# The S5 matrix to the state, formed from transposed and repeated factors

## The chip, the core and the metric

The kernel runs on one core of one Trainium2 chip. The metric is the device time of one execution in microseconds. Below, TensorE is PE (its weight loads PEld), VectorE is DVE, ScalarE is ACT, GpSimd is POOL, and SP is the engine whose queue issues most of the loads.

## The reference, cut to what matters

The program is one step of a two-layer backbone (D 1024, 128 context and 256 latent tokens). Each layer is a feed-forward block (FFN), a mixer of three branches, and a second FFN. One branch of the mixer is a bidirectional S5 layer: 32 groups of 16 channels, 64 complex states per group and direction.

```python
def _s5_direction(u, a_re, a_im, log_dt, b_re, b_im, c_re, c_im, h0, reverse):
    dt = jnp.exp(log_dt)[:, None]
    mag = jnp.exp(a_re * dt)
    abar_r, abar_i = mag * jnp.cos(a_im * dt), mag * jnp.sin(a_im * dt)
    ...
    bbar_r = qr[..., None] * b_re - qi[..., None] * b_im
    bbar_i = qr[..., None] * b_im + qi[..., None] * b_re
    bu_r = jnp.einsum('gph,blgh->blgp', bbar_r, u)
    ...
    _, _, sr, si = lax.associative_scan(_ssm_combine, (ar, ai, bu_r, bu_i), reverse=reverse, axis=1)
    y = jnp.einsum('ghp,blgp->blgh', c_re, sr) - jnp.einsum('ghp,blgp->blgh', c_im, si)
```

## The kernel before

The S5 layer is computed in chunks of TC = 8 steps. Per group it needs three small matrices that depend on the weights alone: ms, from the 8 x 16 inputs of a chunk to the 128 state values (64 states, two directions; real and imaginary part apart), my, from the state to the chunk's outputs, and mi, from the chunk's inputs directly to its outputs. The element of ms for step j, channel h and state s is abar(s) to a power that depends on j, times bbar(s, h). The mixer loads ms with steps and channels (j, h) on the partitions.

These tables are made by a generator, `tables(l)`, that runs beside the first FFN of its layer. Every matrix product of the program is a sequence of weight units (512 rows x 256 columns). After each unit `tick()` advances the tracks: `tables(0)` by 1.9 steps a tick from the eighth tick on, `tables(1)` by 1.6. A step ends at a `yield`. What a step issues on PE stands in PE's queue behind the unit at which it came, since PE's order is written out by hand; the orders of the other engines and queues are set by a planner when the program is built.

`s5_params` runs once, for both layers: it forms pw, the powers 0 to 8 of abar, and writes to DRAM (px_d) two selections of them, one for ms (L866 to L881). `s5_tables(l)` loads both (psx, pyx), runs `s5_rotations`, and then takes four blocks of GB = 8 groups. A block transposes cr to cT on PE, forms bb (bbar, states on the partitions) and two padded copies of operands. It then takes its groups in two halves of GS = 4. For each half VectorE forms my by six operations on 128 x 512 elements and mt, which is ms with the states on the partitions, by another six (L1008 to L1017). Three empty steps follow. Then PE multiplies my with bp and bb (the responses of the chunk, L1024 and L1034, copied to kall), transposes mt eight times (L1047, L138) to tb banks, and ScalarE copies these to ms (L1050), which POOL's queue writes to ms_d. At the block's end kall goes to DRAM, is read in shifted form as mib and written as mi. All DMAs of the tables are issued by POOL's queue; the tiles rotate through the pools c4 (5 buffers), c2 (7) and s1 (7).

A weight unit is loaded by SP's queue to wr, one of 3 buffers (L149), copied by ScalarE to its rounded part wh (L126) and subtracted by VectorE to the low part wl (L105, a line that all two-operand VectorE operations share); wh and wl have 3 buffers each. Three multiplications per tile (L198 to L200) use them. The tracks also load modulation weights modw by SP's queue, which PE multiplies at L386.

Of the kernel before, what the change touches and what calls it, by code (L numbers as in the profile page):

```python
# [56 lines left out]
def hybrid_step(ctx: ExitStack, tc: tile.TileContext, I, pos_r, pos_c, y_prompt, y_sample, new_state):  # L57
# [661 lines left out]
    px_d = [drm.tile([P, 2, 2, TC, G], F32, tag=f"px{l}", name=f"px{l}") for l in range(DEPTH)]  # L719
# [68 lines left out]
    def s5_params(raw, ldt):  # L788
# [81 lines left out]
        lo_i = slice(TC - 1, None, -1), slice(1, TC + 1)  # L870
        hi_i = slice(0, TC), slice(TC, 0, -1)
        for w in range(2):
            px = c4([P, DEPTH, 2, TC, G], "px")
            for i in range(2):
                for rows, ix in ((LO, lo_i[w]), (HI, hi_i[w])):
                    src = pw[rows, i, ix, :].rearrange("p n (l g) -> p l n g", l=DEPTH)
                    for l in range(DEPTH):
                        act.activation(px[rows, l, i], src[:, l], AF.Copy)
            for l in range(DEPTH):
                q.dma_start(px_d[l][:, w], px[:, l])  # L880
# [43 lines left out]
    def s5_tables(l):  # L924
        q = nc.gpsimd
        px = []
        for w in range(2):
            t = c2([P, 2, TC, G], "pxl")
            q.dma_start(t, px_d[l][:, w])
            px.append(t)  # L930
        psx, pyx = px
# [12 lines left out]

        nxt = load_bc(0)
        yield
# [3 lines left out]
        for gb in range(G // GB):  # L950
# [8 lines left out]
            bb = c2([P, 2, GB, 2 * H], "bb")  # L959
            pool.memset(bb, 0.0)  # L960
# [4 lines left out]
            bp = c2([P, 2, GB, 2 * H], "bp")  # L965
            pool.memset(bp, 0.0)
# [4 lines left out]
            ts_(nci, cT[:, 1], -1.0)  # L971
            if gb + 1 < G // GB:
                nxt = load_bc(gb + 1)
            kall = s1([P, 2, 9 * H], "kall")
            for sb in range(GB // GS):
                s0 = sb * GS

                def pexp(tab, i):
                    v = tab[:, i, :, g0 + s0 : g0 + s0 + GS]
                    return v.rearrange("p n g -> p g n").unsqueeze(3).to_broadcast(sh)  # L980
# [5 lines left out]
                b_r, b_i = vec(bb[:, 0]), vec(bb[:, 1])  # L986
                my = c4([P, GS, 2, TC, H], "my")
                t1, t2 = c2(sh, "tp1"), c2(sh, "tp2")
                mul(t1, pexp(pyx, 0), c_r)
                mul(t2, pexp(pyx, 1), c_i)  # L990
# [3 lines left out]
                mul(t1, pexp(pyx, 1), c_r)  # L994
                yield
                mul(t2, pexp(pyx, 0), c_i)
# [21 lines left out]
                for _ in range(3):  # L1018
                    yield
# [830 lines left out]
```

## Time and profile before

| | us |
|---|---|
| median of 3 runs | 1777.1 |
| lowest, highest | 1776.47, 1781.04 |
| time of the profiled execution | 1782.77 |
| its span in the trace | 1780.7 |
| PE busy in the span | 1746.5 |
| DVE, ACT, POOL busy | 1247.1, 794.0, 202.8 |
| bytes moved by DMA | 344.48 MB |

Busy times are unions over one engine's instructions; a matmul's end is modelled and overlaps with the next one's start, so the sum of a group's busy times can be more than what the group adds to the time. In the groups of instructions the number behind the x is the count, then come the busy time and the mean of one, then the idle time of the engine just before them and what ended it. In the timeline a row can merge several instructions in a row of one kind (x8).

### The profile page before, as it was taken

To read this page: it belongs to the slowest core of one execution; us is meant where nothing else is said; L and a number is where in the kernel's file an instruction comes from. 1 tells how busy PE (TensorE), PEld (TensorE's weight loads), DVE (VectorE), ACT (ScalarE), POOL (GpSimd) and SP (SyncE) were. 2 spreads that over 40 slices of the span, in tenths; PEclk is the share of its full clock that TensorE was granted. 3 is DMA by queue.
4 is the path that set the end of the run, shared out by engine and by line. 5 is a ranking of instruction groups with operands and counts; after the bars stand their busy time and mean duration, and the time that the engine had idled before them with its cause. 6 is when DMAs were issued, how large, how long until landed. Compare 5 with 4: busy or idle time off the path is not lost.

```text
span 1780.7 us, 30944 instructions
## 1 busy us (share of the span) xinstructions
PE 1746.5 (98%) x12116; PEld 1654.8 (93%) x12116; DVE 1247.1 (70%) x2344; ACT 794.0 (45%) x1330; POOL 202.8 (11%) x400
## 2 busy tenths in 40 slices
PE   7999999999999999999999999999999999999997
PEld 4899999999899989999999899999989999999997
DVE  4496776778987786679387656767799777544435
ACT  3344333475355553233357233336734646423333
POOL 2012343410010000000001133232100000000000
PEclk8999999999999999999999999999999999999999
DMA  9778788776744577778346777667666443443442
GB/s 329 249 227 273 226 251 270 226 199 185 250 145 131 166 229 224 251 267 265 114 127 208 229 226 213 181 194 232 166 206 195 124 131 119 130 130 121 129 124 77
DMA packets 253753, 344.48 MB, mean 193 GB/s; under 512 B 22399, under 2 KB 216651, under 8 KB 253608
## 3 DMA queue, kind: packets, MB, share of 16 engines
q1 hardware_dynamic: 228504, 299.18, 53.5%
q0 software_dynamic: 17088, 39.51, 7.3%
q10 hardware_dynamic: 8016, 3.82, 0.8%
q8 instruction: 95, 1.56, 0.4%
q14 instruction: 50, 0.41, 0.1%
HBM read 309.75 MB, written 32.70 MB: 192 GB/s over the span
## 4 chain that ended last, share of the span: by engine, by line
PE 84%; DVE 8%; DMA 3%; ACT 3%; issue 1%; SPq 0%; ACTq 0%; DVEq 0%
PE mm L198 26%; PE mm L199 25%; PE mm L200 25%; PE ax L386 3%; DVE wl L105 2%; DVE m_t L105 1%; PE tb L138 1%; DMA modw<-in_w_mod_dram 1%; DVE cacc L123 1%; DVE m_hh L105 1%; PE tb L1249 1%; ACT wh L126 1%; DMA wr<-in_w_in_dram 1%; DMA wr<-in_w_gate_dram 1%; DVE macc L123 1%
## 5 line engine op out<-in xcount | busy, mean ns | idle before, releaser
L105 DVE TENSOR_TENSOR wl<-wr,wh 128x1024 fp32r<-128x1024 f32 (+2 forms) x389 | 457.1, 1176 | 359.8 <-ACT wh L126 354.9
L126 ACT ACTIVATE wh<-wr 128x1024 fp32r<-128x1024 f32 (+1 forms) x387 | 395.5, 1022 | 619.0 <-PE mm L199 452.8
L198 PE MATMUL mm<-hh,wh 128*128 128x384 f32 x1840 | 626.8, 341 | 4.0 <-ACT hh L621 4.0
L200 PE MATMUL mm<-hh,wl 128*128 128x384 f32 x1840 | 617.8, 336 | 1.8 <-DVE wl L105 1.8
L199 PE MATMUL mm<-hl,wh 128*128 128x384 f32 x1840 | 617.4, 336 | 0.2
L198 PEld LDWEIGHTS mm<-hh,wh 128*128 128x128 f32 x1840 | 346.7, 188 | 33.3 <-issue 18.1
L200 PEld LDWEIGHTS mm<-hh,wl 128*128 128x128 f32 x1840 | 346.7, 188 | 3.1 <-DVE wl L105 3.1
L199 PEld LDWEIGHTS mm<-hl,wh 128*128 128x128 f32 x1840 | 346.8, 188 | 1.4 <-DVE hl L105 1.0
L198 PE MATMUL mm<-ah,wh 128*128 128x384 f32 x800 | 271.9, 340 | 0.0
L199 PE MATMUL mm<-al,wh 128*128 128x384 f32 x800 | 269.7, 337 | 1.7 <-DVE al L105 1.7
L200 PE MATMUL mm<-ah,wl 128*128 128x384 f32 x800 | 269.3, 337 | 0.0
L198 PEld LDWEIGHTS mm<-ah,wh 128*128 128x128 f32 x800 | 150.2, 188 | 9.9 <-issue 6.7
L199 PEld LDWEIGHTS mm<-al,wh 128*128 128x128 f32 x800 | 150.2, 188 | 2.0 <-DVE al L105 2.0
L200 PEld LDWEIGHTS mm<-ah,wl 128*128 128x128 f32 x800 | 150.1, 188 | 0.0
L123 DVE SCALAR_TENSOR_TENSOR x<-mm,gt,x 128x128 f32<-128x128 f32 x224 | 83.1, 411 | 33.0 <-PE mm L200 32.7
L198 PE MATMUL mm<-xh,wh 128*128 128x386 f32 x240 | 84.8, 353 | 0.0
L126 ACT ACTIVATE ah<-av 128x384 fp32r<-128x384 f32 x82 | 42.1, 518 | 91.7 <-DVE av L105 91.3
L200 PE MATMUL mm<-xh,wl 128*128 128x386 f32 x240 | 82.1, 342 | 0.0
L199 PE MATMUL mm<-xl,wh 128*128 128x386 f32 x240 | 82.0, 342 | 0.0
L123 DVE SCALAR_TENSOR_TENSOR macc<-modw,silu_c,macc 128x1024 f32<-128x1024 f32 x56 | 69.9, 1278 | 13.8 <-DMA modw<-in_w_mod_dram 13.8
L123 DVE SCALAR_TENSOR_TENSOR cacc<-pad,pv,cacc 128x399 f32<-128x399 f32 x120 | 68.6, 625 | 0.0
L386 PE MATMUL ax<-modw,silu_c 128*32 128x512 f32 (+1 forms) x576 | 62.6, 514 | 0.4 <-DMA modw<-in_w_mod_dram 0.4
(316 smaller groups left out, 1820.4 us busy)
## 6 DMA issues: line engine op xcount, KB each, us to landing
wr<-in_ffn_w_dram SPq DMA_DIRECT2D x256, 512.0 KB, 3.6
modw<-in_w_mod_dram SPq DMA_DIRECT2D x144, 512.0 KB, 5.0
wr<-in_w_gate_dram SPq DMA_DIRECT2D x48, 512.0 KB, 4.3
wr<-in_w_in_dram SPq DMA_DIRECT2D x24, 512.0 KB, 3.6
my<-my POOLq DMA_DIRECT2D x16, 512.0 KB, 5.5
ms<-ms POOLq DMA_DIRECT2D x16, 512.0 KB, 4.9
m_ms<-ms SPq DMA_DIRECT2D x16, 512.0 KB, 4.7
m_my<-my SPq DMA_DIRECT2D x16, 512.0 KB, 10.6
```

The source lines that it names most:

```text
L105: (eng or dve).tensor_tensor(out, a, b, op=op)
L123: dve.scalar_tensor_tensor(out, a, s, b, op0=op0, op1=op1)
L126: act.activation(hi, full, AF.Copy)
L138: pe.transpose(out, in_, ident[:rows, :rows])
L198: pe.matmul(out, wh[:, k, cols], xh, start=first, stop=False)
L199: pe.matmul(out, wh[:, k, cols], xl, start=False, stop=False)
L200: pe.matmul(out, wl[:, k, cols], xh, start=False, stop=last)
L386: pe.matmul(b[32 * s : 32 * s + 32, :w], silu_c[:, k, :], raws[i][:, c : c + w], start=(k == 0), stop=(k == KD - 1), skip_group_check=True,)
L1249: pe.matmul(b[64 * half : 64 * half + NCH, g * P : (g + 1) * P], u, w, start=(n == 0), stop=(n == 2), skip_group_check=True,)
```

## The change

ms is no longer formed with the states on the partitions and transposed on PE per half block. Its two factors are transposed instead: the powers once (pw, in `s5_params`, eight transposes), and bbar once per block (bc, two transposes, `factor_rows`). Both are written to DRAM (pt_d, bt_d) and repeated there by DRAM-to-DRAM copies to the rows (j, h): the powers over the channels (ptr_d, four copies in `s5_params`), bbar over the steps (btr_d, one copy per block). Each half block loads its 4 groups of both (pt, bt) and VectorE forms ms directly, by six operations on 128 x 512 elements. px_d holds only the selection for my. The steps of a block are reordered: both halves' my first, the responses of the first half during the second half's my, then the two loads, the responses of the second half, and the two halves of ms. The clears of bb and bp (`padded`) move one block ahead. The steps of a block are 16 instead of 17; `s5_params` has four more.

```diff
-    px_d = [drm.tile([P, 2, 2, TC, G], F32, ...
+    px_d = [drm.tile([P, 2, TC, G], F32, ...
+    pt_d = [drm.tile([2, TC, G, P], F32, ...
+    bt_d = [drm.tile([H, G, 2, P], F32, ...
+    ptr_d = [drm.tile([TC, H, 2, G * P], F32, ...
+    btr_d = [drm.tile([TC, H, G, 2 * P], F32, ...
...
+        pws = c4([P, TC, P], "pws")
+        for i in range(2):
+            b = tb_bank()
+            for m in range(TC // 2):
+                transpose(
+                    b[:, m * P : (m + 1) * P], pw[:, i, 2 * m : 2 * m + 2, :].rearrange("p n r -> p (n r)"), P
+                )
+            bv = b.rearrange("p (m s) -> p m s", s=P)
+            o = pws[:, 4 * i : 4 * i + 4]
+            act.activation(o[:, ::-1, LO], bv[:, :, LO], AF.Copy)
+            act.activation(o[:, :, HI], bv[:, :, HI], AF.Copy)
+            yield
+        for n2 in range(2):
+            for l in range(DEPTH):
+                r = n2 * NG + l * G
+                rows_d = pt_d[l].rearrange("i j g s -> (i j) g s")
+                for half, off in ((LO, 1 - n2), (HI, n2)):
+                    q.dma_start(
+                        rows_d[off::2, :, half].rearrange("m g s -> g m s"), pws[r : r + G, :, half]
+                    )
+        yield
+        for l in range(DEPTH):
             for i in range(2):
+                src = pt_d[l][i].rearrange("j g s -> j (g s)").unsqueeze(1).to_broadcast([TC, H, G * P])
+                q.dma_start(ptr_d[l][:, :, i], src)
         yield
...
+        def padded():
+            t = [c2([P, 2, GB, 2 * H], nm) for nm in ("bb", "bp")]
+            for v in t:
+                pool.memset(v, 0.0)
+            return t
...
+            bc = s1([P, 2, GB, H], "bc")
+            act.activation(bc, bb[:, :, :, :H], AF.Copy)
...
+            def factor_rows():
+                b = tb_bank()
+                for i in range(2):
+                    transpose(b[:, i * P : (i + 1) * P], bc[:, i].rearrange("p g h -> p (g h)"), P)
+                bts = s1([P, 2, P], "bts")
+                act.activation(bts.rearrange("p i s -> p (i s)"), b[:, : 2 * P], AF.Copy)
+                q.dma_start(bt_d[l][:, gs].rearrange("h g i s -> g h (i s)"), bts.rearrange("r i s -> r (i s)"))
+                src = bt_d[l][:, gs].rearrange("h g i s -> h g (i s)").unsqueeze(0)
+                q.dma_start(btr_d[l][:, :, gs], src.to_broadcast([TC, H, GB, 2 * P]))
...
-                mt = c4([P, GS, 2, TC, H], "mt")
-                t1, t2 = c2(sh, "tp1"), c2(sh, "tp2")
-                mul(t1, pexp(psx, 0), b_r)
...
-                for _ in range(3):
-                    yield
...
+            def to_rows_in(sb):
+                gr = slice(g0 + sb * GS, g0 + (sb + 1) * GS)
+                pt = c4([P, 2, GS * P], "pt")
+                cols_ = slice(gr.start * P, gr.stop * P)
+                q.dma_start(pt, ptr_d[l].rearrange("j h i x -> (j h) i x")[:, :, cols_])
+                bt = c4([P, GS, 2 * P], "bt")
+                q.dma_start(bt, btr_d[l].rearrange("j h g x -> (j h) g x")[:, gr])
...
+            def to_rows(sb):
+                pt, bt = ins[sb]
+                ms = c4([P, GS, 2, P], "ms")
+                t1, t2 = (c2([P, GS, P], f"tp{i}") for i in (1, 2))
+                mul(t1, pt[:, 0], bt[:, :, 0])
+                mul(t2, pt[:, 1], bt[:, :, 1])
                 yield
+                sub(ms[:, :, 0], t1, t2)
+                t1, t2 = (c2([P, GS, P], f"tp{i}") for i in (1, 2))
+                mul(t1, pt[:, 0], bt[:, :, 1])
                 yield
+                mul(t2, pt[:, 1], bt[:, :, 0])
+                add(ms[:, :, 1], t1, t2)
+                q.dma_start(ms_d[l][:, g0 + sb * GS : g0 + (sb + 1) * GS], ms)
+                yield
...
-                ms = c4([P, GS, 2, P], "ms")
-                for g2 in range(0, GS, 2):
-                    b = tb_bank()
-                    for j in range(4):
-                        transpose(
-                            b[:, j * P : (j + 1) * P], mt[:, g2 + j // 2, j % 2].rearrange("p i h -> p (i h)"), P
-                        )
-                    act.activation(ms[:, g2 : g2 + 2].rearrange("p g r c -> p (g r c)"), b, AF.Copy)
-                q.dma_start(ms_d[l][:, g0 + s0 : g0 + s0 + GS], ms)
+            mys, ins = [], []
+            yield
+            for n, _ in enumerate(from_rows(0)):
+                if n == 1:
+                    factor_rows()
+                yield
+            for n, _ in enumerate(from_rows(1)):
+                if n == 0:
+                    responses(0)
+                yield
+            to_rows_in(0)
+            yield
+            to_rows_in(1)
+            yield
+            responses(1)
+            if gb + 1 < G // GB:
+                pads = padded()
+            yield from to_rows(0)
+            yield from to_rows(1)
```

## Rows read from the trace of the kernel before

**Rows 1.** The page: busy PE, and the span in 40 slices of 44.5 us.

```profile
PE 1746.5 (98%) x12116; PEld 1654.8 (93%) x12116; DVE 1247.1 (70%) x2344; ACT 794.0 (45%) x1330; POOL 202.8 (11%) x400
DMA  9778788776744577778346777667666443443442
GB/s 329 249 227 273 226 251 270 226 199 185 250 145 131 166 229 224 251 267 265 114 127 208 229 226 213 181 194 232 166 206 195 124 131 119 130 130 121 129 124 77
```

**Rows 2.** The page: the chain that ended last, by engine, shares of the span.

```profile
PE 84%; DVE 8%; DMA 3%; ACT 3%; issue 1%; SPq 0%; ACTq 0%; DVEq 0%
```

**Rows 3.** Stretches of 10 us: busy PE, PEld, DVE, ACT, POOL, clock, DMA, GB/s.

```profile
140.00:150.00 10.00, 10.00 (x60) 8.91 (x59) 4.37 (x8) 6.14 (x10) 4.89 (x13) 1.00 0.98 337
150.00:160.00 10.00, 10.00 (x61) 8.91 (x60) 2.77 (x3) 3.08 (x5) 0.00 (x0) 1.00 1.04 385
230.00:240.00 10.00, 10.00 (x59) 10.00 (x58) 8.93 (x15) 3.16 (x5) 3.11 (x6) 1.00 1.04 394
```

**Rows 4.** Waits: who waited for whom; us in total, times, longest.

```profile
SPq L149 <- DVE wl L105: 1085.9, 324, 8.0
ACT wh L126 <- PE mm L199: 452.8, 217, 5.1
```

**Rows 5.** Chain in order of time near 350 us: start us, us, what.

```profile
350.35 10.31 DMA wr<-in_w_in_dram
```

**Rows 6.** Timeline, one burst of table matmuls: start us, duration us, engine, line.

```profile
182.27 0.34 PE L200 MATMUL mm<-hh,wl 128*128 128x384 f32 x1
182.54 0.65 PE L1024 MATMUL tb<-my,bp 128*32 128x128 f32 x16
183.22 1.24 PE L138 MATMUL tb<-ident,mt 128*128 128x128 f32 x8
184.22 0.42 PE L198 MATMUL mm<-hh,wh 128*128 128x384 f32 x1
```

**Rows 7.** Groups of instructions, whole span: busy us, mean ns of one, idle before.

```profile
L138 PE MATMUL tb<-ident,mt 128*128 128x128 f32 x128 | 19.3, 287 | 0.0
L1050 ACT ACTIVATE ms<-tb 128x512 f32<-128x512 f32 x32 | 17.9, 598 | 2.5 <-PE tb L138 2.5
L105 DVE TENSOR_TENSOR mt<-tp,tp 128x512 f32<-128x512 f32 x32 | 21.9, 685 | 0.2
L105 DVE TENSOR_TENSOR tp<-pxl,bb 128x512 f32<-128x512 f32 x64 | 42.5, 685 | 0.4
L958 ACT ACTIVATE cT<-tb 128x256 f32<-128x256 f32 x8 | 2.9, 368 | 0.9 <-PE tb L138 0.9
```

**Rows 8.** Timeline around the transposes that begin a block of eight groups.

```profile
162.93 0.34 PE L200 MATMUL mm<-hh,wl 128*128 128x384 f32 x1
163.10 0.38 PE L138 MATMUL tb<-ident,cr 128*128 128x128 f32 x2
163.24 0.42 PE L198 MATMUL mm<-hh,wh 128*128 128x384 f32 x1
```

**Rows 9.** Timeline of POOL, before the first block of layer 0.

```profile
124.35 0.71 POOL L938 DMA_DIRECT2D braw<-in_s_b_re_dram  x1
127.64 0.56 POOL L929 DMA_DIRECT2D pxl<-px  x1 [2.58 <-DMA px<-px]
```

**Rows 10.** Timeline, VectorE and ScalarE: the first output matrix of that block.

```profile
164.09 0.37 ACT L958 ACTIVATE cT<-tb 128x256 f32<-128x256 f32 x1
165.97 1.89 DVE L105 TENSOR_TENSOR tp<-pxl,cT 128x512 f32<-128x512 f32 x3
171.02 0.68 DVE L123 SCALAR_TENSOR_TENSOR my<-tp,tp 128x512 f32<-128x512 f32 x1
```

**Rows 11.** DMA issues: count, KB each, median us from issue to landing.

```profile
my<-my POOLq DMA_DIRECT2D x16, 512.0 KB, 5.5
m_my<-my SPq DMA_DIRECT2D x16, 512.0 KB, 10.6
mib<-kd POOLq DMA_DIRECT2D x64, 64.0 KB, 5.2
```

More of the change, by code (lines that the diff above doesn't have):

```diff
@@ L718, in hybrid_step @@
     rho_d = [drm.tile([P, 4, G // 4, NE], F32, tag=f"rhod{l}", name=f"rhod{l}") for l in range(DEPTH)]
-    px_d = [drm.tile([P, 2, 2, TC, G], F32, tag=f"px{l}", name=f"px{l}") for l in range(DEPTH)]
+    px_d = [drm.tile([P, 2, TC, G], F32, tag=f"px{l}", name=f"px{l}") for l in range(DEPTH)]
+    pt_d = [drm.tile([2, TC, G, P], F32, tag=f"pt{l}", name=f"pt{l}") for l in range(DEPTH)]
+    bt_d = [drm.tile([H, G, 2, P], F32, tag=f"bt{l}", name=f"bt{l}") for l in range(DEPTH)]
+    ptr_d = [drm.tile([TC, H, 2, G * P], F32, tag=f"ptr{l}", name=f"ptr{l}") for l in range(DEPTH)]
+    btr_d = [drm.tile([TC, H, G, 2 * P], F32, tag=f"btr{l}", name=f"btr{l}") for l in range(DEPTH)]
     NG = DEPTH * G
@@ L868, in s5_params @@
             yield
[L870 to L873, printed above, removed]
-            for i in range(2):
[L875 to L880, printed above, removed]
+        px = c4([P, DEPTH, 2, TC, G], "px")
+        for i in range(2):
+            for rows, ix in ((LO, slice(1, TC + 1)), (HI, slice(TC, 0, -1))):
+                src = pw[rows, i, ix, :].rearrange("p n (l g) -> p l n g", l=DEPTH)
+                for l in range(DEPTH):
+                    act.activation(px[rows, l, i], src[:, l], AF.Copy)
+        for l in range(DEPTH):
+            q.dma_start(px_d[l], px[:, l])
+        yield
[12 more added lines that the diff above has]
+        for n2 in range(2):
+            for l in range(DEPTH):
+                r = n2 * NG + l * G
[5 more added lines that the diff above has]
+        yield
+        for l in range(DEPTH):
+            for i in range(2):
+                src = pt_d[l][i].rearrange("j g s -> j (g s)").unsqueeze(1).to_broadcast([TC, H, G * P])
+                q.dma_start(ptr_d[l][:, :, i], src)
         yield
@@ L925, in s5_tables @@
         q = nc.gpsimd
[L926 to L931, printed above, removed]
+        pyx = c2([P, 2, TC, G], "pxl")
+        q.dma_start(pyx, px_d[l])
         def load_bc(gb):
@@ L993, in s5_tables @@
                 t1, t2 = c2(sh, "tp1"), c2(sh, "tp2")
[L994 removed]
+                mul(t1, pexp(1), c_r)
                 yield
[L996 removed]
+                mul(t2, pexp(0), c_i)
                 stt(
```

32 lines of the change are left out of this document (16 added, 16 removed).

## Prediction

> **What bounds the kernel now.** I read the page first. TensorE is busy for 1746.5 of 1780.7 us [rows 1], and the chain that ended last lies on it for 84% of the span [rows 2]. VectorE (70%) and ScalarE (45%) have room on the whole. Then I looked at the stretches in which the tables are made, some 100 to 340 us for layer 0 and 1000 to 1215 us for layer 1. In the 10 us windows there TensorE is busy 10.00 of 10.00 [rows 3]. So in these stretches a microsecond of TensorE work that goes is a microsecond of time, as long as weights, VectorE's low halves and the tables' own operands go on arriving before TensorE needs them. That they do now is seen in who waits: ScalarE's weight split waits 452.8 us for TensorE to free a buffer, and the weight queue 1085.9 us for VectorE to free one [rows 4]. Supply waits for TensorE, not the other way round. The third view is DMA: the slices that hold layer 0's tables, the fourth to eighth of 44.5 us, move 273, 226, 251, 270 and 226 GB/s [rows 1], mean 249, and single windows reach 385 and 394 GB/s while TensorE still runs without a gap [rows 3]. So about 140 GB/s are free there on average. That this has an end shows at 350 us, where the chain stands on one weight transfer for 10.31 us [rows 5].
>
> **What goes.** The 128 transposes of mt go. In one burst they begin at 183.22 and the next weight multiplication at 184.22 [rows 6], so eight of them hold TensorE for 1.00 us. 128 of them have 19.3 us of busy time [rows 7], but that overlaps with the multiplications behind. 16 bursts at 1.00 us are 16.0 us; by the busy time it would be up to 19.3. With them go 32 evictions of ms, 17.9 us of ScalarE [rows 7]; nobody on the path waited for those, so I give them nothing.
>
> **What comes on TensorE.** Two transposes of bc in each of eight blocks: the cr transposes are the same thing, 162.93 to 163.24 where the next multiplication would have begun at some 163.10 (spacing 0.17), plus the longer start behind it, so about 0.3 us [rows 8], 2.4 us for eight. Once, eight transposes of pw in two bursts, about 1.2 us. Net on TensorE: 16.0 - 2.4 - 1.2 = 12.4 us less.
>
> **VectorE and ScalarE.** The to-state matrix still takes six operations on 128x512 per four groups. Those with broadcast operands cost 685 ns, those with plain ones 685 ns too [rows 7], so the new layout changes nothing. ScalarE gets bc and bts, eight of each of 128x256 at 0.37 us as cT [rows 7], some 6 us, and loses 17.9. The two clears move ahead of their block; they are POOL work on which nothing on the path waits. These edits I cost at nothing; what hides them is TensorE's weight multiplications.
>
> **What comes on DMA.** ptr_d is 2.1 MB per layer and part, four copies, 8.4 MB in one go at about 140 us; btr_d is 1.05 MB per block, 8.4 MB in eight; pt and bt are read back, 512 KB each per four groups, 16.8 MB. That is 33.6 MB more. No row of before shows a DRAM-to-DRAM copy. If it costs as much as a load of its bytes at 390 GB/s [rows 3], the first 8.4 MB are 21.5 us of all 16 engines; if reading and writing count one after the other, 43 us. Their price in time is 0 if they fit in the 140 GB/s that are free, for they are then only spread over 60 us and more. At the other end they take the engines alone for 43 us. A unit is 24 multiplications, and 60 fit in 10 us [rows 3], so 4 us; three raw and about two split tiles lie ahead of TensorE, so supply may be late by some 14 us before TensorE stops, and the loss is 43 - 14 = 29 us. It can't be below nothing, since no transfer that now holds up TensorE in this stretch becomes smaller. The windows with 385 and 394 GB/s and no gap are the nearest rows, so I take 3 us. By the Trainium skill, page "DMA: Bandwidth & Descriptors", section "Latency and other measured facts", copies of 16 KiB rows between HBM tensors run at up to 214 GB/s a direction; by that estimate the 8.4 MB are 39 us, near my upper end, and no row here shows it.
>
> In POOL's queue the eight pt_d writes wait for ScalarE and the four copies wait for those writes. Behind them stand the loads of the first block, the rotation writes and the bc loads. The first block's turn comes some 10 us later than before (four more steps of the generator), and POOL's order already sets loads that wait for nothing ahead of waiting ones (braw ahead of the second pxl, which waits for px to land) [rows 9], so I cost this wait at nothing; if the loads do queue behind 43 us of copies, it is inside the 29 us above.
>
> **The new chain in each block.** Two waits of TensorE and VectorE are new. First, the response matmuls of the first four groups are now issued one step after my is complete, where it was six. A step is (182.54 - 163.10) / 8 = 2.4 us [rows 6, 8]. my was finished 171.70 - 163.10 = 8.6 us after the block's first transposes [rows 8, 10], and TensorE now comes after four steps, 9.7 us. That just fits: 0 to 1 us a block, I take 0.25, so 2 us. Second, VectorE's to-state multiplications need bt. From the transposes of bc: ScalarE 1.4 us (cT ends at 164.46, its transposes began at 163.10 [rows 8, 10]), the write of bt_d 5.2 to 5.5 us, the copy 5.5 to 21.2 us (a 512 KB transfer, or twice the slow one), the load 5.5 to 10.6 us [rows 11]: 18 to 39 us, middle 28. The program gives it seven steps, 17 us; VectorE is about 4 us behind its place anyway (171.70 against one tick after 163.10) and the split tiles give about 6 us more, 27 in all. So at the middle nothing or 1 us is lost, at the upper end 12 us a block. Behind the waiting multiplication stand the low halves of the weights and the evictions, so what exceeds the cover stops TensorE. I take nothing.
>
> **Sum.** -12.4 + 3 + 2 = -7.4 us. On the profiled execution that is 1782.8 to 1775.4; its span is 2.1 us shorter than its time, and it lies 5.7 us above the median of 1777.1. On the median: 1769.7, rounded to 1770.
>
> **Rivals.** (1) The traffic eats the gain: the first copies take twice their bytes and win the engines from the weight tiles, which costs another 5 to 12 us, 1775 to 1782, about 1778. For it speaks that the chain does stand on a weight transfer at 350 us [rows 5]; against it, that 394 GB/s pass without a gap [rows 3]. (2) Slower: VectorE stands at the to-state multiplications of each block because bt comes late. Price: with a chain of 31 us instead of 28, 4 us over the cover in each of eight blocks, 32 us, so 1777 - 12 + 32 = 1797. It decides from a chain of 27 us on. For it: four dependent transfers in a row, m_my loads that take 10.6 us [rows 11]; against it: short, wide rows and an idle queue on the POOL side. (3) Copies on half of the engines: both copies have the eight steps as outermost dimension, and if only eight engines share one, it runs at 195 GB/s; the block's copy takes 5.4 to 10.8 us, the first four 43 to 86 us if they fall on the same eight, and each weight tile, which lies on all engines, waits for the busy ones. With 35% of that lost and 14 us of cover, 1 to 16 us, plus 1 or 2 us a block: about 1785. The Trainium skill says this in "DMA: Bandwidth & Descriptors", section "Rules for kernel authors": an outermost dimension of fewer than 16 confines the whole DMA to at most so many engines; the trace of before has no such copy. That the change doesn't do what it says I give no chance: the transposes are gone in the code.
>
> **How the numbers follow.** Forecast 0.49, 1763 to 1773; traffic 0.18; late chain 0.22; half of the engines 0.11. The range takes in the full 12.4 us and a little more of TensorE's busy time, 1761, and reaches to the late chain's 1797, beyond which about 1 in 10 is left. A measurement of this kernel can tell 0.3%, 5.3 us. Faster by more: nearly all of the forecast's case, 0.48. Within: most of the traffic case and the forecast's edge, 0.21. Slower: the last two, 0.31.
>
> **What would show it.** Right: no transposes of mt, bursts of TensorE that are 1 us shorter, TensorE still at 10.00 of 10.00 from 150 to 340 us, 0.4 us or less of waiting at the response matmuls. Wrong: VectorE idle before the to-state multiplications with a DMA of bt as its releaser, TensorE waiting for the weight split at 140 to 200 us, windows above 390 GB/s with gaps in TensorE, or blocks of tables that follow each other more slowly.

## The result, and the profile after

| | before | after |
|---|---|---|
| median, us | 1778.53 (4 runs) | 1886.31 (4 runs) |
| lowest to highest | 1776.47 to 1781.04 | 1884.60 to 1888.54 |
| span of the profiled execution | 1780.7 | 1883.9 |
| TensorE busy in it | 1746.5 | 1763.9 |

The change makes the kernel slower: the ratio is 1.060, interval 1.0584 to 1.0616. The forecast was 1770 in a range up to 1797. All transposes of mt are gone (12012 instructions of PE where there were 12116), and yet PE is busy for longer. The page of the changed kernel says where (busy time, then PE, its clock and DMA in 40 slices of 47.1 us; before: [rows 1]):

```profile
PE 1763.9 (94%) x12012; PEld 1666.9 (88%) x12012; DVE 1247.7 (66%) x2344; ACT 781.4 (41%) x1310; POOL 239.3 (13%) x456
PE   7997877889989999999999989889999999999998
...
PEclk9998888899999999999999999899899999999999
DMA  9769867869665557678534877565777434434432
GB/s 340 247 200 343 279 197 243 290 218 233 201 213 144 159 158 255 213 265 270 177 114 156 257 274 259 180 218 180 224 198 239 140 113 135 123 123 130 128 118 84
```

Between the first slice and the last, PE is busy for less than 90% in the fourth to ninth and the twelfth (layer 0's tables and what follows them) and in the 24th, 26th and 27th (layer 1's tables); its granted clock is under 0.9 in the fourth to eighth, the 26th and the 29th. To see how much each part loses I took the start of the n-th weight multiplication (L198 to L200, 8832 recorded) in both traces. Up to the 481st, at 131 us of before, the changed kernel is 1.5 us ahead; it then falls behind by 69.1 us until the 4897th (1013 us of before), and by 35.6 us more from there to the end. Nearly all of it falls into the stretches of the tables.

Two kinds of loss are seen. The first is at 160 to 190 us, during and just behind the four first copies, which are issued at 138 to 140 us and have all landed at 172 us (busy PE, PEld, DVE, ACT, POOL, clock, DMA share, GB/s in stretches of 10 us):

```profile
150.00:160.00 10.00, 10.00 (x61) 8.91 (x60) 1.23 (x1) 0.98 (x2) 1.25 (x4) 1.00 0.98 343
160.00:170.00 10.00, 7.40 (x39) 5.77 (x37) 1.23 (x1) 1.44 (x2) 0.70 (x3) 0.98 0.96 329
170.00:180.00 10.00, 1.92 (x4) 0.18 (x4) 0.00 (x0) 0.56 (x1) 0.00 (x0) 0.50 1.04 409
180.00:190.00 10.00, 9.20 (x37) 8.66 (x38) 7.22 (x15) 5.83 (x11) 1.27 (x3) 0.66 0.84 286
```

From 170 to 180 us the DMA engines are full (1.04, 409 GB/s) and the compute engines nearly stand. The copies have the room that the weight tiles had in [rows 3]. From 150 to 160 us SP's queue (q1) moved 3.62 MB in the kernel before and 0.58 MB in the changed one, where POOL's (q0) moved 2.85 MB (packets, MB, share of 16 engines):

```profile
q1 hardware_dynamic: 1933, 3.62, 96.9%
...
q0 software_dynamic: 462, 2.85, 77.6%
q1 hardware_dynamic: 465, 0.58, 20.4%
```

TensorE waits 2.1 and 3.7 us for modulation weights there, and 5.0 us for the weight split. The second kind is in the blocks of the tables (who waited for whom; us in total, times, longest):

```profile
ACT wh L126 <- DMA wr<-in_ffn_w_dram: 51.2, 7, 17.7
PE tb L138 <- ACT bc L1001: 30.2, 5, 11.0
PE tb L1084 <- DVE my L105: 24.3, 4, 7.4
DVE tp L105 <- DMA bt<-btr: 5.1, 1, 5.1
```

TensorE waits for bc, that is for bb, at the new transposes, and for my at the responses; both are made by VectorE. VectorE itself waited for bt only once, for 5.1 us. The timeline of PE shows what such a wait does beside its own length:

```profile
312.15 0.69 PE L138 MATMUL tb<-ident,bc 128*128 128x128 f32 x2 [10.75 <-ACT bc L1001]
...
313.27 0.52 PE L200 MATMUL mm<-ah,wl 128*128 128x384 f32 x1
313.59 0.52 PE L198 MATMUL mm<-ah,wh 128*128 128x384 f32 x1
...
316.80 0.34 PE L200 MATMUL mm<-ah,wl 128*128 128x384 f32 x1
316.97 0.34 PE L198 MATMUL mm<-ah,wh 128*128 128x384 f32 x1
```

```profile
312.00:316.00 4.00, 3.85 (x13) 3.85 (x14) 4.00 (x6) 1.04 (x2) 4.00 (x8) 0.50 0.82 197
320.00:324.00 4.00, 4.00 (x46) 3.97 (x35) 3.96 (x7) 0.00 (x0) 2.33 (x5) 1.00 0.90 276
```

After the wait the multiplications follow each other at 0.32 us, at 0.17 us some four microseconds later; the granted clock of 312 to 316 us is 0.50, the lower of its two levels (1.2 GHz), and 1.00 from 320 us on.

### The profile page after: what moved, and what is told of

It reads as the page before. It is cut to its first block, busy times and chain, and to the rows that moved or that the text cites. A ratio compares the mean times of both kernels' runs of the same rounds, so it can differ in the third digit from the quotient of the medians.

```text
span 1883.9 us, 30791 instructions
## 1 busy us (share of the span) xinstructions
PE 1763.9 (94%) x12012; PEld 1666.9 (88%) x12012; DVE 1247.7 (66%) x2344; ACT 781.4 (41%) x1310; POOL 239.3 (13%) x456
## 4 chain that ended last, share of the span: by engine, by line
PE 70%; DVE 8%; DMA 2%; issue 2%; ACT 1%; POOL 0%; DVEq 0%; SPq 0%; ACTq 0%; POOLq 0%
PE mm L198 22%; PE mm L199 21%; PE mm L200 21%; DVE wl L105 2%; PE ax L386 1%; DVE tp L105 1%; DMA modw<-in_w_mod_dram 1%; DVE m_t L105 1%; PE tb L1320 1%; DVE cacc L123 1%; DVE macc L123 1%; DVE ms L105 1%; DVE m_hh L105 1%; PE tb L1084 0%; DMA bt<-btr 0%
## 5 line engine op out<-in xcount | busy, mean ns | idle before, releaser
L198 PE MATMUL mm<-hh,wh 128*128 128x384 f32 x1840 | 633.4, 344 | 9.0 <-ACT wh L126 5.0
L200 PE MATMUL mm<-hh,wl 128*128 128x384 f32 x1840 | 623.1, 339 | 2.7 <-DVE wl L105 2.7
L198 PEld LDWEIGHTS mm<-hh,wh 128*128 128x128 f32 x1840 | 351.3, 191 | 39.4 <-issue 17.7
L200 PEld LDWEIGHTS mm<-hh,wl 128*128 128x128 f32 x1840 | 351.0, 191 | 4.6 <-DVE wl L105 4.5
L199 PEld LDWEIGHTS mm<-hl,wh 128*128 128x128 f32 x1840 | 351.2, 191 | 1.5 <-DVE hl L105 1.1
L198 PE MATMUL mm<-ah,wh 128*128 128x384 f32 x800 | 274.7, 343 | 0.0
L200 PE MATMUL mm<-ah,wl 128*128 128x384 f32 x800 | 271.2, 339 | 0.0
L198 PEld LDWEIGHTS mm<-ah,wh 128*128 128x128 f32 x800 | 152.2, 190 | 11.2 <-issue 8.3
L200 PEld LDWEIGHTS mm<-ah,wl 128*128 128x128 f32 x800 | 151.9, 190 | 0.0
L198 PE MATMUL mm<-xh,wh 128*128 128x386 f32 x240 | 85.5, 356 | 0.0
L200 PE MATMUL mm<-xh,wl 128*128 128x386 f32 x240 | 82.8, 345 | 0.0
L123 DVE SCALAR_TENSOR_TENSOR macc<-modw,silu_c,macc 128x1024 f32<-128x1024 f32 x56 | 70.0, 1278 | 12.4 <-DMA modw<-in_w_mod_dram 12.4
## 6 DMA issues: line engine op xcount, KB each, us to landing
ptr<-pt POOLq DMA_DIRECT2D x4, 2048.0 KB, 23.8
btr<-bt POOLq DMA_DIRECT2D x8, 1024.0 KB, 10.1
```

The costliest lines, as they stand in the source:

```text
L123: dve.scalar_tensor_tensor(out, a, s, b, op0=op0, op1=op1)
L198: pe.matmul(out, wh[:, k, cols], xh, start=first, stop=False)
L199: pe.matmul(out, wh[:, k, cols], xl, start=False, stop=False)
L200: pe.matmul(out, wl[:, k, cols], xh, start=False, stop=last)
```

## The experiments

The table holds all runs; the ratio is to runs of the kernel before on the same chip. The last two columns are the change in lag behind the kernel before between the 481st and the 4897th weight multiplication (layer 0) and from there to the end (layer 1), from the profiled execution. "Left out" marks runs whose pt or bt is not the real factor or whose ms is not turned.

| run | median us | ratio (95%) | layer 0 | layer 1 |
|---|---|---|---|---|
| changed kernel | 1886.3 | 1.060 (1.058 to 1.062) | +69.1 | +35.6 |
| no_transposes (left out) | 1763.0 | 0.991 (0.989 to 0.993) | -8.3 | -8.3 |
| no_bt_wait (left out) | 1880.4 | 1.056 (1.054 to 1.059) | +62.9 | +35.8 |
| sixteen | 1869.7 | 1.051 (1.049 to 1.053) | +53.5 | +32.9 |
| spread | 1884.2 | 1.060 (1.057 to 1.063) | +62.9 | +35.8 |
| deferred | 1912.7 | 1.074 (1.072 to 1.077) | +89.2 | +40.7 |
| direct | 1874.1 | 1.053 (1.051 to 1.055) | +57.8 | +35.8 |
| far | 1903.8 | 1.070 (1.068 to 1.072) | +70.7 | +47.6 |
| far_direct | 1882.7 | 1.058 (1.056 to 1.059) | +56.4 | +44.7 |
| near_free (left out) | 1772.8 | 0.996 (0.995 to 0.998) | -2.3 | -8.7 |
| far_free (left out) | 1771.3 | 0.995 (0.993 to 0.997) | -6.7 | -7.2 |
| bt_direct_far | 1857.2 | 1.043 (1.042 to 1.045) | +52.2 | +22.8 |
| far_direct_sp | 1819.2 | 1.023 (1.021 to 1.025) | +34.6 | +1.5 |
| first_only (left out) | 1799.0 | 1.012 (1.010 to 1.013) | +21.2 | -6.4 |
| block_only (left out) | 1861.3 | 1.046 (1.044 to 1.047) | +38.2 | +42.2 |
| block_idle (left out) | 1851.9 | 1.042 (1.040 to 1.043) | +36.5 | +37.6 |
| early_loads | 1822.2 | 1.025 (1.024 to 1.027) | +38.7 | +0.5 |
| block_ready (left out) | 1816.9 | 1.021 (1.019 to 1.023) | +35.5 | -7.9 |
| repeat_on_write | 1799.8 | 1.011 (1.010 to 1.013) | +26.4 | -6.3 |

**What the transposes are worth.** In the kernel before:

```diff
-                        transpose(b[:, j * P : (j + 1) * P], mt[:, g2 + j // 2, j % 2]...
-                    act.activation(ms[:, g2 : g2 + 2]..., b, AF.Copy)
-                q.dma_start(ms_d[l][...], ms)
+                q.dma_start(ms_d[l][...], mt...)
```

> The kernel before, without the 128 transposes of mt and the 32 evictions of ms: mt goes to DRAM as it stands, not turned, so this part of the computation is left out. It measures the gain that the change aims at by itself. If TensorE bounds the tables as my sum had it, the time falls by about 16 us (16 bursts of 1.00 us), to some 1762 us, in 16 steps of 1 us. If the supply of weights is nearly as late as TensorE, part of that comes back as waits: 5 us or less is gained.

Measured: 1763.0 against 1779.6, 16.6 us, and the lag falls in sixteen steps to -17.4 us. The first term of the sum stands.

**Is it the wait for bt?**

```diff
-                q.dma_start(bt, btr_d[l].rearrange("j h g x -> (j h) g x")[:, gr])
+                q.dma_start(bt, ptr_d[l].rearrange("j h i x -> (j h) i x")[:, 0, old]...)
```

> The changed kernel, with bt loaded from the first copies (ptr_d), which are ready long before, in place of the block's own copy; the block's copy still runs, but nobody waits for it, so the bytes moved are the same and the product is not the reference's matrix. Theory A (the chain bc, bts, copy, load is late and VectorE stands at the to-state multiplications): the 78 us of the eight blocks go nearly all, and what is left is the burst of the first copies at 150 to 212 us, some 25 us per profile: about 1800 to 1810 us. Theory B (what costs is where the 12 to-state operations stand on VectorE, ahead of the next block's my and bb, whether bt is late or not): less than a third of the 78 us goes, 1865 or more.

Measured: 6 us less, which is theory B's side. TensorE now waits 49.1 us for bc although VectorE waits 3.4 us for bt.

**The form and the place of the copies.** sixteen puts the channels first in both copies; spread makes the first copies in eight parts, a block ahead. (This holds for layer 0's. Layer 1's parts wait for nothing, and POOL issued them from 359 to 584 us, long before layer 1.)

```diff
-   src = pt_d[l][i]....unsqueeze(1).to_broadcast([TC, H, G * P])
+   src = pt_d[l][i]....unsqueeze(0).to_broadcast([H, TC, G * P])   (sixteen; btr in the same way)
-   q.dma_start(ptr_d[l][:, :, i], src)
+   q.dma_start(ptr_d[l][:, :, i, c], src)                          (spread, at the start of the block before)
```

> The changed kernel with both repeat copies written with the 16 channels as their outermost dimension in place of the 8 steps. If an outermost dimension of 8 confines a copy to half of the engines (rival 3 of the prediction), the block's copy (1024 KB, 10.1 us from issue to landing now) lands in 5 to 6 us and the first four (2048 KB each, 23.8 us) in some 12 to 15 us, and the time falls by some 20 to 50 us. If the copies already use all engines, landings and time stay within 1% (1886 us).

> The changed kernel with the first copies (8.4 MB in one go at 140 us) cut into eight parts of 1 MB, each made one block ahead. If the burst costs the 25 us that the weight multiplications fall behind between 150 and 212 us, that step shrinks to 5 us or less and the time is about 1860 us. If those 25 us come from something else (the order on VectorE or ScalarE at the first block), the step stays and the time is within 5 us of 1886. If the traffic of the blocks already is at its limit, the steps of the blocks grow by 1 to 3 us each and eat up the gain.

The DMA issues (count, KB each, median us from issue to landing), of the changed kernel and of sixteen:

```profile
ptr<-pt POOLq DMA_DIRECT2D x4, 2048.0 KB, 23.8
btr<-bt POOLq DMA_DIRECT2D x8, 1024.0 KB, 10.1
bt<-btr POOLq DMA_DIRECT2D x16, 512.0 KB, 7.9
```

```profile
ptr<-pt POOLq DMA_DIRECT2D x4, 2048.0 KB, 19.3
btr<-bt POOLq DMA_DIRECT2D x8, 1024.0 KB, 7.9
```

sixteen: landings a fifth shorter, not half, and 17 us of time, of which about 5 lie at the waits for weights and the rest in the blocks. With eight outermost a copy here is slower, but its landing isn't twice as long. spread: TensorE no longer waits for weights at 160 to 181 us, and the blocks of layer 0 lose some 10 us more. But a second part of the burst's step stays, 8 us at the responses of the first block. It isn't the burst: the first of TensorE's two waits there is the same in the changed kernel and, below, in repeat_on_write, where no weight is late:

```profile
202.42 0.66 PE L1084 MATMUL tb<-my,bp 128*32 128x128 f32 x8 [4.30 <-DVE my L105]
...
187.09 0.66 PE L1088 MATMUL tb<-my,bp 128*32 128x128 f32 x8 [4.30 <-DVE my L105]
```

It is 4.30 us in spread, first_only and block_ready too: VectorE's order has my behind two more low halves of weights there than in near_free, which waits 1.3 us.

**More time for the chain, or no copies.** deferred makes the loads and the twelve to-state operations of a block one block later; direct takes the copies out and loads 16 partitions at a time; far puts TensorE's uses far behind VectorE.

```diff
+            if late:
+                yield from late[1](0)         (deferred: the block before's operations here)
+                yield from late[1](1)
...
+                for j in range(TC):           (direct)
+                    q.dma_start(pt[r], pv[j].unsqueeze(0).to_broadcast([H, 2, GS * P]))
+                    q.dma_start(bt[r], bv)
...
+                yield from late[1](0)         (far: responses six steps behind my)
+            responses(0)
```

> The changed kernel, with the loads of pt and bt and the twelve to-state operations of a block made one block later, so that the chain from bc to bt has a whole block (some 45 us) and not seven steps. The uses by TensorE (transposes of bc one step after bb, responses one step after my) stay where they are. Chain theory: the waits for bt go and with them most of the 78 us, about 1810 us. Order theory: TensorE's new uses of bb and my still stand behind VectorE's queue, in which the to-state operations and the low halves of later weights come first; less than half of the loss goes, 1845 us or more.

> The changed kernel without the DRAM-to-DRAM copies: pt and bt are loaded from pt_d and bt_d in eight loads of 16 partitions each, so the repeating is done by the loads. 16.8 MB of traffic and one of the four transfers of the chain go, and there is no burst at 140 us; POOL issues 32 loads a block where it issued 4. If the copies are the cause (burst and chain), about 1800 us. If the order on VectorE is, the burst's 25 us go and the blocks keep their steps or take a part of it back: 1850 to 1875 us.

> The changed kernel with the copies as they are, but with all of TensorE's new uses put as far behind VectorE as in the kernel before: the responses six steps after my, the transposes of bc five steps after bb, the to-state operations one block later (pt and bt then take their buffers from the ring of four that the core uses later). Order theory: the steps at the blocks go except where the copies still hold up the loads, and what is left is the first copies' burst of 25 us and some waits behind it: 1800 to 1820 us. Traffic theory (the copies' bytes cost the time wherever the uses stand): 1850 us or more.

> Both together: no DRAM-to-DRAM copies, and TensorE's uses as far behind VectorE as before. If order and copies are the two causes and nothing else is, TensorE's 16 us (measured: 16.7 us) less the 2.4 and 1.2 us of the new transposes come out: about 1767 us, 12 us under the kernel before. If a third cause is left (the half clock by itself, the loads of 16 partitions), 1780 us or more.

By the numbers deferred and direct came out on the order theory's side (1845 or more, 1850 to 1875), far on the traffic theory's, far_direct on a third cause's. But that deferred and far would be slower than the changed kernel nobody expected. direct has no copies and no burst, and its blocks lose as much as the changed kernel's, with TensorE waiting 70.8 us for bc. far_direct loses nearly as much in all, although from 100 to 310 us it has no wait of TensorE and is 5.9 us ahead of before. What stops it is in its timeline of POOL, and then of PE:

```profile
287.95 0.54 POOL L1054 DMA_DIRECT2D pt<-pt  x1
...
322.11 0.51 POOL L1055 DMA_DIRECT2D bt<-bt  x1
...
327.32 0.54 POOL L966 MEMSET bb<- 128x512 f32 x1
```

```profile
331.82 0.69 PE L138 MATMUL tb<-ident,bc 128*128 128x128 f32 x2 [24.79 <-ACT bc L996]
```

POOL needs 34 us for 32 issues of loads (0.51 us each, the rest waits in between), and the clear of the next bb comes behind them.

**No repeating at all.** So the layout and the repeating were parted: pt and bt as whole tiles from a weight matrix.

```diff
-                q.dma_start(pt, ptr_d[l]...)
+                q.dma_start(pt, other[:P, ...])
...
-                q.dma_start(bt, btr_d[l]...)
+                q.dma_start(bt, other[P : 2 * P, ...])
...
-                q.dma_start(ptr_d[l]..., src)
-                q.dma_start(btr_d[l]..., src)
```

> The changed kernel with the repeating left out: no DRAM-to-DRAM copies, and pt and bt are loaded as whole tiles of the same size from a weight matrix that is always there. So the to-state operations wait for nothing that is late, and the bytes of the copies go too; TensorE's transposes of bc and its responses stay one step behind bb and my. If the nearness of these uses costs by itself (VectorE's queue puts low halves of later weights ahead of bb and my), the blocks still fall behind by 5 us each or more: 1800 to 1830 us. If the copies and their chain are the whole cause, about 1767 us.

> As the run before it (the repeating left out, pt and bt from a weight matrix), but TensorE's uses six steps behind my and five behind bb, and the to-state operations a block later. It bounds what this layout can give here: if order and copies are all, TensorE's 16.7 us less the 3.6 us of the new transposes, 1766 us; the half clock does not appear since TensorE never stands. If 1780 us or more, something else in the new layout costs (the two extra loads, VectorE's order).

near_free is 6.3 us under the kernel before by the medians, 12.6 by the two traces; far_free is no better than it by more than the interval. So the change without the repeating gains, by the medians about half of what the sum said, and TensorE's near uses cost nothing while the data are there and VectorE's order is near_free's. Near uses by themselves are not the cause. The 113.5 us between 1772.8 and 1886.3 belong to the repeating: the copies and what hangs on them.

**Which copies.**

```diff
first_only:  bt from the weight matrix, no copies to btr_d
block_only:  pt from the weight matrix, no copies to ptr_d
block_idle:  as block_only, bt from the weight matrix too (the copies run, nobody waits for them)
block_ready: as block_idle, and the copies' source:
-                src = bt_d[l][:, gs].rearrange("h g i s -> h g (i s)").unsqueeze(0)
+                src = I["w_out"][l][2 * P : 2 * P + 32]....unsqueeze(0)
```

> The changed kernel with the first copies (8.4 MB at 140 us) as they are, but without the copies of the blocks: bt is loaded from a weight matrix, so the repeating of bt is left out. With neither copy the kernel took 0.9961 of the time before. If the first copies cost the 25 us of their burst, 1773 + 25 = about 1798 us. If part of that is won back later in layer 0 because the blocks no longer wait, 1780 to 1790 us.

> The other half: the copies of the blocks and the whole chain from bc to bt as they are, but no first copies; pt is loaded from a weight matrix, so the repeating of pt is left out. If the blocks' chain is the main cause, the eight steps of some 10 us stay: 1773 + 78 = about 1850 us, more if the 25 us of the burst only move into the blocks (1870 us).

> As block_only, but bt too is loaded from a weight matrix, so that nobody waits for the blocks' copies; they still run and still stand in POOL's queue, each waiting there for its write of bt_d to land, ahead of the loads of pt and bt, the clear of the next bp and the writes of the kernels. If VectorE's wait for bt is the mechanism (rival 2 of the prediction), about 1773 us, as without copies. If it is the copies' place in POOL's queue and the order that the planner makes for it (clear of bp late, bb late, low halves first), nearly all of the 78 us stays: 1840 us or more.

> As block_idle (no first copies, pt and bt loaded from a weight matrix, the repeating left out), but the blocks' copies read from a weight matrix too, so that they move the same 8.4 MB from the same place in POOL's queue and wait there for nothing. block_idle took 1852 us and the kernel without copies 1773. If the wait in POOL's queue for the write of bt_d (and VectorE's order that the planner makes for what stands behind it) is the cause, about 1775 us. If the bytes are, 1840 us or more.

The first copies cost 1799.0 - 1772.8 = 26.2 us, the blocks' copies 1861.3 - 1772.8 = 88.5; together 114.7, measured 113.5. Of the 88.5, only 9.4 are there because someone waits for bt (1861.3 - 1851.9).

block_ready was to part the bytes from the dependence, and doesn't. Its copies wait for nothing, so they were not issued from the same place: three go out in the first 23 us, the others at 150, 203, 322, 380 and 423 us, none in layer 1, where block_idle has four from 1050 us on. The last of them:

```profile
423.04 0.62 POOL L1008 DMA_DIRECT2D btr<-in_w_out_dram  x1
```

So its layer 1 has no copies and gains 7.9 us as the kernel without copies does, and its layer 0 has all of them. The 35.0 us between the two (1851.9 - 1816.9) are no price of the dependence alone. What block_idle's loss consists of, its waits say:

```profile
PE tb L138 <- ACT bc L996: 48.0, 5, 11.0
PE ax L138 <- ACT modev L396: 15.7, 4, 7.3
ACT modev L396 <- DVE ms L105: 16.0, 3, 7.6
```

In near_free the first two are 1.3 and 0.5 us. modev (the modulation's evicted product) shares a ring of seven buffers with the operands of the to-state operations, and its eviction waits for VectorE's ms. Busy PE and the rest in 200 us of layer 1 (1050 to 1250 us), changed kernel, block_idle, near_free:

```profile
sum 200.00, PE 172.46 PEld 157.58 DVE 113.45 ACT 55.38 POOL 61.58; mean PE 43.11 PEld 39.40 DVE 28.36 ACT 13.85 POOL 15.39
```

```profile
sum 200.00, PE 170.73 PEld 159.93 DVE 110.16 ACT 54.55 POOL 67.53; mean PE 42.68 PEld 39.98 DVE 27.54 ACT 13.64 POOL 16.88
```

```profile
sum 200.00, PE 199.93 PEld 191.88 DVE 148.25 ACT 89.06 POOL 63.84; mean PE 49.98 PEld 47.97 DVE 37.06 ACT 22.27 POOL 15.96
```

How a copy for which nobody waits can cost this is seen on VectorE. Timeline of block_idle in layer 1, then of its POOL and PE:

```profile
1091.58 1.23 DVE L105 TENSOR_TENSOR wl<-wr,wh 128x1024 fp32r<-128x1024 f32 x1 [2.27 <-ACT wh L126]
1092.72 1.89 DVE L105 TENSOR_TENSOR tp<-pt,bt 128x512 f32<-128x512 f32 x3
...
1099.34 0.28 DVE L105 TENSOR_TENSOR bb<-cm,cm 128x128 f32<-128x128 f32 x1
1099.54 0.68 DVE L105 TENSOR_TENSOR ms<-tp,tp 128x512 f32<-128x512 f32 x1
1100.15 0.28 DVE L105 TENSOR_TENSOR bb<-cm,cm 128x128 f32<-128x128 f32 x1
```

```profile
1097.31 0.57 POOL L1070 DMA_DIRECT2D ms<-ms  x1 [25.29 <-DVE ms L105]
```

```profile
1101.59 0.69 PE L138 MATMUL tb<-ident,bc 128*128 128x128 f32 x2 [11.01 <-ACT bc L996]
```

POOL has nothing to do for 25 us, so the loads are long issued, and VectorE does not wait for bt. But the twelve to-state operations stand in its queue behind the low half of a weight unit (wl, which waits for ScalarE's wh) and directly ahead of the second block's bb, for which TensorE stands. In layer 1 of block_ready, without copies, the same operations end 13 us ahead of bb:

```profile
1125.57 0.69 DVE L105 TENSOR_TENSOR ms<-tp,tp 128x512 f32<-128x512 f32 x1
1138.93 0.28 DVE L105 TENSOR_TENSOR bb<-cm,cm 128x128 f32<-128x128 f32 x1
```

The order is in the program, not found at run time. Counting low halves in VectorE's queue, the first block's to-state operations stand behind the 36th to 39th in near_free, and bb of the second block behind the 40th. In the changed kernel, no_bt_wait, spread, block_only, block_idle and direct the operations stand behind the 43rd, and bb with them. In layer 1 it is the 219th to 222nd and bb behind the 225th, against the 227th for both. Each of these six loses 35.6 to 42.2 us in layer 1; first_only, block_ready and repeat_on_write, whose to-state operations end ahead of bb there as near_free's do, gain. One of the six, direct, has no copies, and in two nobody waits for the copies' data. So the loss in layer 1 goes with this order, and its waits show how. Why the planner sets it isn't shown. It came with the write, the copy and the load in a row, and with 32 issues in POOL's queue. It did not come with repeat_on_write's write and load. POOL's real wait ahead of the copies was 16.1 us in six times in block_idle, spread over both layers.

In layer 0 it is less clean, but the waits are of the same kind. block_ready loses 35.5 us there. 14.9 of them come at 498 us, where TensorE waits 12.5 us for m_hh of the core, which stands later on VectorE, and about 20 in the blocks, where it waits for my: my stands behind the 35th, 44th and 60th low half in the first, second and fourth block, in near_free behind the 33rd, 41st and 58th. In all of layer 0's column TensorE waits for no DMA. A further 6 us, not in the column, lie ahead of the tables, where three copies run and TensorE waits 4.4 us for modulation weights. Whether the planner chose layer 0's order because of the copies' bytes is open; no run shows it.

**Versions with the real factors.** far_direct_sp moves pt's loads to SP and the clears to VectorE; bt_direct_far has pt from copies and bt loaded straight; early_loads has the loads at the start of the next block.

```diff
-                    q.dma_start(pt[r], ...)            (far_direct_sp)
+                    nc.sync.dma_start(pt[r], ...)
...
+                for j in range(TC):                    (bt_direct_far)
+                    q.dma_start(bt[j * H : (j + 1) * H], bv)
...
+            if late:                                   (early_loads, ahead of a block's first step)
+                late[0](0)
+                late[0](1)
```

> TensorE's uses far behind VectorE, pt from copies that are made one block ahead (16 channels outermost), bt loaded straight from bt_d in eight loads of 16 partitions, the clears of bb and bp on VectorE. POOL issues 20 transfers a block for it where the version with both loaded straight issued 32 and fell behind by 34 us. If POOL's issue queue was what stopped that version at the fourth block, this one stays ahead: 1765 to 1785 us. If not, 1840 us or more.

> No DRAM-to-DRAM copies, uses far, pt and bt by loads of 16 partitions, but the sixteen loads of pt of a block are issued by SP in place of POOL, and the clears of bb and bp run on VectorE. If POOL's queue was the stop, POOL is relieved by half: 1765 to 1785 us, unless the weight loads that stand behind pt's loads in SP's queue come late, which would show as waits of the weight split for a load. If POOL's queue was not the stop, 1840 us or more.

> No copies, uses far, pt's loads on SP, clears on VectorE, and now the loads of a block at the start of the next (the last block's ahead of its own writes), so that POOL has the bt loads out before the kernels' writes queue up. The version without this lost 33 us at the end of layer 0, where VectorE stood 22.7 us for the last bt, and 6 us at the fourth block. If POOL's queue was the reason, both go: 1770 to 1780 us. If the loads of 16 partitions are slow in themselves, 1800 us or more.

All three are slower than was expected of them if POOL's queue was the stop (1765 to 1785 us, early_loads 1770 to 1780). But with POOL relieved, layer 1 loses 1.5 and 0.5 us in far_direct_sp and early_loads instead of 44.7: there POOL's queue was far_direct's stop. What is left lies at the end of layer 0: in far_direct_sp VectorE stands 22.7 us for the last bt, ahead of the residual; in early_loads the loads of the core's sgw come late in POOL's queue and TensorE waits 29.2 us for them. bt_direct_far loses in both layers (TensorE waits 18.0 us for sgw, 17.6 for bc).

Last, the repeating in the write itself, without a copy:

```diff
-                q.dma_start(bt_d[l][:, gs].rearrange("h g i s -> g h (i s)"), bts....)
-                src = bt_d[l][:, gs]....unsqueeze(0)
-                q.dma_start(btr_d[l][:, :, gs], src.to_broadcast([TC, H, GB, 2 * P]))
+                src = bts.rearrange("r i s -> r (i s)").unsqueeze(1).to_broadcast([P, TC, 2 * P])
+                q.dma_start(btr_d[l][gb].rearrange("j h g x -> (h g) j x"), src)
...
+        if l:
+            repeat_powers(l, 0, 4)      (layer 1's first copies, in the program at the start of its tables)
```

> The changed kernel with three edits: bts is written to btr_d eight times over by one transfer from SBUF (rows in the order channel, group), so the write of bt_d, the wait for it in POOL's queue and the copy go; layer 1's first copies are made at the start of layer 1's tables; the first copies have 16 channels outermost. If POOL's wait is what cost 79 us and the burst is in proportion to its bytes (4.2 MB in place of 8.4), the blocks cost nothing and the burst some 10 us: 1775 to 1790 us. If the bytes of the blocks' repeating cost, 1840 us or more.

1799.8 us, 10 us above the upper end that was expected, 86.5 under the changed kernel, and still 1.1% over the kernel before. Layer 1 gains 6.3 us with real data, the repeated writes of its blocks and the near uses. Its first copies are not in it: they wait for nothing but pt_d, and POOL issued them at 197 and 277 us, in layer 0's tables. From 1050 to 1250 us the DMA engines' share is 0.78 to 0.97 in stretches of 50 us, in block_idle 0.61 to 0.77; so in layer 1 it is not the traffic that costs. Busy times of this stretch, and the repeated write's landing:

```profile
sum 200.00, PE 199.95 PEld 190.58 DVE 141.91 ACT 76.89 POOL 76.58; mean PE 49.99 PEld 47.65 DVE 35.48 ACT 19.22 POOL 19.14
```

```profile
btr<-bts POOLq DMA_DIRECT2D x8, 1024.0 KB, 7.0
```

Layer 0 still loses 26.4: some 8 at the first block's responses, the rest in the other blocks; TensorE's new waits are for my, bc and bts. All first copies lie there, but only half of their bytes at 140 us, and TensorE no longer waits for weights there.

## Why the prediction was wrong, step by step

- **What bounds the kernel, and what goes.** Right for the transposes: 16.0 us were named, 16.6 measured. The net of 12.4 is near_free's by the two traces (12.6), but by the medians it gains 6.3 (interval 4.4 to 9.4), about half; what takes the rest isn't shown.
- **First copies: 3 us, bounds 0 to 29.** Mis-sized; with them the kernel takes 26.2 more. By the traces of first_only and near_free 14 of these are the waits for weights that the term was meant for, and 9 come at the first block's responses, from VectorE's order, which was in no term. The value was taken from the wrong rows: the 385 GB/s [rows 3] are weight loads (3.62 MB of 3.85), and of the 394 GB/s SP's loads are 185 and POOL's transfers 209. They show what the engines can move, not room beside the weights. The upper bound also has a slip: five tiles of 4 us are 20 us of cover, not 14.
- **Responses one step after my: 2 us.** Right by itself: near_free waits 1.3 us at them. The 26 us in the changed kernel (24.3 in the row above, 1.8 in one more) come with VectorE's other order.
- **The chain of bt: nothing, upper end 12 us a block.** This is the step that failed: 88.5 us for eight blocks, 11.1 a block. The length was no surprise: landings of 3.2, 10.1 and 7.9 us (write, copy, load) make some 21 of the 28 taken. What failed is how it costs. I weighed it against a cover of 27 us as if VectorE's order stayed, and asked what stands behind a waiting multiplication. The order is made anew, and a late chain in it moves the twelve operations next to the following bb, on which the change has put TensorE with a slack of two steps. So the price is paid also when no one waits for the data: 9.4 us are the wait, and the other 79.1 are there in block_idle, where TensorE stands 48.0 us for bc and 15.7 for modev, both behind the to-state operations; the rest I put down to the lower clock after such waits. Why the order came out so, and what part of it the copies' bytes have in layer 0, stays open.
- **Rival 2** (VectorE stands at the to-state multiplications, 1797, chance 0.22) had the side and the place right and the mechanism wrong: VectorE stood 5.1 us for bt, TensorE 54.5 us for bb and my (and 16.1 for modev).
- **Rival 3** (half of the engines, 1785). The Trainium skill, "DMA: Bandwidth & Descriptors", "Rules for kernel authors", says that fewer than 16 outermost confine a copy. sixteen agrees in the sign, 23.8 to 19.3 and 10.1 to 7.9 us, but not in a factor of two; 17 us of 108, most of them in the blocks, where VectorE's order is not quite the changed kernel's either. Which engines a copy used, no trace here shows.
- **Rival 1** (traffic eats the gain, 1778) was the first copies' case, with 5 to 12 us where the waits for weights cost some 14.
- **The clock** was in no term. In before it is 1.00 in all these stretches. In the changed kernel it falls after the waits. In layer 1's 200 us TensorE is idle for 27.5 us, and up to the end for 31 us more than in near_free, while the loss against near_free is 35.6 + 8.7 = 44.3; the difference of some 13 I put down to multiplications at the lower level, which no run measures by itself.
- **The signs** that were to show it wrong did appear (TensorE waiting for the split, windows above 390 GB/s with gaps), save the one on VectorE. The range, up to 1797, took in one case at a time; burst, chain and clock came together.

## What to carry to other kernels

Where a planner sets an engine's order, a longer chain into one operation can also move its neighbours: ask which operation then stands next to it and who waits for that one, not only whether the data come in time. Repeat data in the write that is needed anyway rather than by a copy behind it (1799.8 against 1886.3 us, with the first copies changed too); repeating in loads of 16 partitions was no way out here (1874.1). And look in the trace when a transfer really ran before naming what a run parts: a copy that waits for nothing moved from layer 1 into layer 0. Room on the DMA engines is what is left beside the loads in that stretch; a window that loads and writes due there already fill is no evidence for room.

## What the runs showed of the hardware

A wait of TensorE is paid again in its clock: after 10.75 us of standing the multiplications came at 0.32 us with a granted clock of 0.50, then at 0.17 again. A load of 16 partitions (64 KB) took 6.6 to 6.9 us to land in direct, about as long as one of 512 KB in whole rows (7.9); 32 of them in far_direct kept POOL's queue for 34 us, half of it in issuing (0.51 us each). Writing 128 KB from SBUF eight times over by one transfer landed in 7.0 us, where the write and the copy took 3.2 and 10.1.
